# Sixteen early landing places, one modulation path moved between engines, and a feed-forward finish by quarters in a one-core decoder layer

## The chip, the core and the metric

The kernel runs on one core of a Trainium2 chip. TensorE multiplies matrices, VectorE (DVE) and ScalarE (ACT) work elementwise, GpSimd (POOL) here only fills memory with zeros, and SyncE (SP) issues the transfers from main memory. The metric is device time in microseconds (us) of one execution.

## The reference

One layer of a decoder trunk, batch 1, 256 tokens, width 2048, all in float32:

```
mod = silu(c) @ w_ada + b_ada                 # 2048 -> 12288: sh1, sc1, g1, sh2, sc2, g2
h   = rms_norm(x, norm1_g) * (1 + sc1) + sh1
q, k, v, u = split(h @ w_in)                  # 2048 -> 4096
attn = dilated_attention(rms(q), rms(k), v)   # 8 heads of 128, three dilations
y    = gelu(s5(u))                            # 64 groups, 64 complex states, a scan
ssm  = y * sigmoid(y @ w_glu + b_glu)
x    = x + g1 * (concat(rms(attn), rms(ssm)) @ w_out)
h2   = rms_norm(x, norm2_g) * (1 + sc2) + sh2
out  = x + g2 * (relu(h2 @ w_ff1)**2 @ w_ff2) # 2048 -> 8192 -> 2048
```

## The kernel before

**Weights.** All weights stream through once, some 300 MB. A weight tile of 512 KB lands in one of five buffers called raw; ScalarE copies it to wh (a rounded high part), VectorE writes raw - wh to wl, and TensorE computes high x high, high x low and low x high (the split, lines 161 and 136; lines 193 to 195 in the input projection). wh and wl have three buffers each. A part is 1 MB of w_in (two raw tiles, 24 matmuls of 512 columns) or 512 KB of w_out, w_ff1 or w_ff2. A part of the latter is 24 matmuls of 256 columns in `pair_bank` (lines 869 to 872, both outputs in one PSUM bank) or 8 of 512 and 8 of 256 in `pair_part` (lines 860 and 862).

**Modulation.** w_ada, 100 MB, is cut into 24 blocks of four 1 MB pieces; a block gives four columns of 128 of `mod`. `ADA_ORDER` is the order of the blocks. A block in `PE_BLOCKS` goes to TensorE: per piece four matmuls of 32 output columns (line 254), at the end a copy, four transposing matmuls (line 265) and an add into `mod`. Any other block goes to VectorE: each piece is multiplied by silu(c) and summed (line 158); silu(c), copied to all partitions, is the tile cbc, which is loaded and computed near the start. `pump(n)` issues the next n pieces; `pump_at(i)` issues `PUMPS[i]` of them on average at each part of stage i. The first eight pieces land in tiles that are not used yet (Q, K, U, V, and two halves each of TO and CA), later ones in the tags of the current ring (`RINGS`), or in raw in two halves.

**The order of the work.** The text of the program: eight pieces of modulation, small S5 terms, h(0), the input projection in blocks of 512 columns n and groups of 512 rows kg (h(kg) is made by `make_h`), and between its blocks the tables of the S5 branch: `b_step` and `ca_step` on VectorE, `pad_write` copies on ScalarE into the zeroed tiles padB (PD) and padCs (WB0, WB1), `toep_half` (TensorE line 526), `wb_block`. When u is complete, `state_in` and `scan` (VectorE, tiles XT and T0) run beside the rest of the input projection; then `y_block` (lines 697 and 701), attention and w_glu, the output projection from both branches, the second norm (n, line 828 broadcasts it), h2, and the feed-forward. There `ff1_half(0)` and `ff1_half(8)` run the first two groups of rows for 16 column pairs and store the partial sums in part; ff1(0) to ff1(7) finish eight of them pair by pair, then ff1 and ff2 alternate in four groups G.

The compiler orders the instructions of each engine by its own simulation, with the text as priority; every engine then works its queue in that order. `tc.issue_after(x)` keeps instructions behind x.

In the listing, acc and tr are PSUM tiles (four banks each).

Of the kernel before, what the change touches and what calls it, by code (L numbers as in the profile page):

```python
# [9 lines left out]
F32 = mybir.dt.float32  # L10
# [6 lines left out]
P = 128  # L17
# [9 lines left out]
RAW = 5  # L27
RINGS = (('Q', 'K'), ('raw',), ('T0', 'PD', 'raw', 'raw'), ('T0', 'raw', 'raw'), ('raw',), ('HA', 'U', 'WB0'), ('HA', 'PD'))
PUMPS = (2.0, 2.0, 1.0, 1.0, 1.0, 1.0, 1.0, 0.5, 0.5, 2.5, 1.0, 2.0, 1.0, 0.5)

# [10 lines left out]
SUB = [0, 2, 1, 3]  # L41
PE_BLOCKS = (0, 1, 4, 5, 10, 11, 12, 16)
ADA_ORDER = (4, 0, 5, 1, 6, 2, 7, 3, 8, 9, 10, 11, 12, 16, 13, 17, 14, 18, 15, 19, 20, 21, 22, 23)

# [153 lines left out]
def _body(nc, tc, I, out, sb, ps):  # L198
# [14 lines left out]
    c0 = t("T0", [P, 2, 32, 16])  # L213
    cbc = t("cbc", [P, DM])
    ones = t("ones", [P, 1])
# [8 lines left out]
    mod = t("mod", [P, 96])  # L224
    first = [t(tag, [P, 4, NB]) for tag in ("Q", "K", "U", "V")]
    for tag in ("TO", "CA"):
        w = t(tag, [P, 8, NB])
        first += [w[:, 0:4], w[:, 4:8]]

    ring = {"tags": ("raw",), "i": 0, "first": 0}  # L230

    def ada_raw(src):
        if ring["first"] < 8:
            raw = first[ring["first"]]
            ring["first"] += 1
            nc.sync.dma_start(raw, src.rearrange("p (a n) -> p a n", a=4))
            return [raw]
        ring["i"] += 1
        tag = ring["tags"][ring["i"] % len(ring["tags"])]
        if tag not in ("raw", "T0"):  # L240
            raw = t(tag, [P, 4, NB])
            nc.sync.dma_start(raw, src.rearrange("p (a n) -> p a n", a=4))
            return [raw]
        return [k.raw(src[:, 2 * NB * i : 2 * NB * i + 2 * NB].rearrange("p (a n) -> p a n", a=2), tag) for i in range(2)]

    def ada_pieces(b):
# [20 lines left out]
        else:  # L267
            part = t("adap", [P, 2, 4], bufs=2)
            for j in range(4):
                o = 0  # L270
                for i, raw in enumerate(ada_raw(I["w_ada"][b, j])):
                    n = raw.shape[1] * NB
                    rf = raw.rearrange("p a n -> p (a n)")
                    stt(rf, rf, 1.0, cbc[:, o : o + n], ALU.mult, ALU.mult, accum=part[:, i, j : j + 1])
# [42 lines left out]
    def make_h(kg):  # L317
# [3 lines left out]
        for kc in range(4 * kg, 4 * kg + 4):  # L321
            v = xTf[:, kc]
            mul(v, v, rbc)
            nc.scalar.activation(v, v, AF.Identity, bias=mod[:, kc : kc + 1], scale=g1c[:, kc : kc + 1])
            end = k.split(hs[kg][:, 0, kc % 4], hs[kg][:, 1, kc % 4], v)
        return end.ins
# [150 lines left out]

    padB = t("PD", [P, 32, 2, 2, 16])
    padCs = [t(f"WB{i}", [P, 8, 2, 2, 4, 16]) for i in range(2)]
    for w in (padB, *padCs):  # L480
        nc.gpsimd.memset(w, 0.0)
    by_r = lambda v: v.rearrange("p i r j -> p r i j")
# [128 lines left out]
    for i in range(4):  # L611
        sl = slice(NB * i, NB * i + NB)
        sg = t("rows", [P, NB], bufs=2)
        with tc.issue_after(h_act):
            nc.scalar.activation(sg, cbc[:, sl], AF.Sigmoid)
        with tc.issue_after(h_end):
            mul(cbc[:, sl], cbc[:, sl], sg)
    with tc.issue_after(h_act):
# [10 lines left out]
    make_h(1)  # L629
    ring["tags"] = RINGS[1]  # L630
    cw = t("T0", [P, 2, 2, 16, 16])
# [9 lines left out]
    s5_powers()  # L641
    ring["tags"] = RINGS[2]
    run(w_in_pair(4, [0, 1]), 3)
# [4 lines left out]
    make_h(3)  # L648
    ring["tags"] = RINGS[3]
    for n in (0, 1):  # L650
        run(w_in_block(n, [3]), 6)
    ring["tags"] = RINGS[4]
    u2 = t("PD", [P, 2, 32, 32])
# [145 lines left out]
    for n in range(2):  # L799
# [20 lines left out]
        if n == 0:  # L820
            ring["tags"] = RINGS[6]
            att = t("U", [P, NH, SEQ])
# [119 lines left out]
    def ff1_half(base):  # L942
# [7 lines left out]
        for i in range(8):  # L950
            copy(part[base + i], banks[i])

    def ff1(np_):
        pp = [k.acc(), k.acc()]
# [3 lines left out]
        for kg in kgs:  # L958
            pair_part(pp, I["w_ff1"][np_, kg], h2[4 * kg : 4 * kg + 4], kg == kgs[0], kg == 3)
        aa = ff1_slot(np_)  # L960
        v = t("rows", [P, 2, SEQ], bufs=2)
        for e in range(2):
# [70 lines left out]
```

## Time and profile before

| | |
|---|---|
| median of 3 runs | 1297.09 us (1292.63 to 1297.53) |
| the profiled execution | 1291.11 us, span 1289.3 us |
| TensorE (PE) busy | 1193.7 us, 93% of the span |
| weight loads (PEld) | 1012.5 us, 79% |
| VectorE busy | 910.5 us, 71% |
| ScalarE busy | 579.0 us, 45% |
| moved by transfers | 299.64 MB, mean 232 GB/s |
| mean granted TensorE clock | 0.948 of full |

[...] The profile's other views give the same by stretches of time, by line, or as a list in order of time.

### The profile page before, as it was taken

The numbers are of one execution on the slowest core, as the hardware profiler recorded it, in microseconds if no ns is written. First come the engines' busy times: TensorE is split into PE (matmuls) and PEld (weight loads), VectorE is DVE, ScalarE is ACT, GpSimd is POOL, SyncE is SP. The second block draws the span as 40 slices with busy tenths as digits, with TensorE's granted clock in tenths as the row PEclk, the third lists the DMA queues.
The fourth block names the chain that finished last, engine by engine and source line by source line (L and its number), as shares of the span: only waits on it lengthen the run. The fifth ranks groups of instructions, "written<-read, shape, count | busy, mean of one in ns | idle before, by whom it ended". The sixth has DMA issues, their size and how long they took to land.

```text
span 1289.3 us, 18892 instructions
## 1 busy us (share of the span) xinstructions
PE 1193.7 (93%) x7330; PEld 1012.5 (79%) x7330; DVE 910.5 (71%) x1499; ACT 579.0 (45%) x792; POOL 13.0 (1%) x12
## 2 busy tenths in 40 slices
PE   4688899998998799789989999999999999999998
PEld 1456677863777699789978888888888888888887
DVE  5977697899534985668799655975576666667564
ACT  3588644332145544334354444453344443344432
POOL 1100000000000000000000000000000000000000
PEclk9798999997679899989999999999999999999999
DMA  9785898779155665658997666766677666767663
GB/s 371 286 317 186 280 333 287 274 267 385 36 179 180 239 193 175 210 182 297 327 326 252 203 191 216 262 212 182 195 236 240 225 187 190 219 222 227 202 212 95
DMA packets 77705, 299.64 MB, mean 232 GB/s; under 512 B 8624, under 2 KB 10928, under 8 KB 71856
## 3 DMA queue, kind: packets, MB, share of 16 engines
q1 hardware_dynamic: 77616, 298.45, 69.1%
q8 instruction: 57, 0.93, 0.3%
q14 instruction: 32, 0.26, 0.0%
HBM read 296.31 MB, written 2.10 MB: 231 GB/s over the span
## 4 chain that ended last, share of the span: by engine, by line
PE 60%; DMA 15%; DVE 15%; ACT 5%; issue 4%; SPq 0%; ACTq 0%; DVEq 0%
PE acc L860 31%; PE acc L862 15%; DMA raw<-w_ada 10%; DVE wl L136 4%; DVE raw L158 3%; DVE T L136 2%; PE acc L872 2%; PE acc L870 2%; PE acc L869 2%; PE acc L701 1%; DMA raw<-w_ff 1%; ACT wh L161 1%; PE acc L697 1%; DVE XT L136 1%; ACT TO L161 1%
## 5 line engine op out<-in xcount | busy, mean ns | idle before, releaser
L161 ACT ACTIVATE wh<-raw 128x1024 fp32r<-128x1024 f32 x360 | 381.3, 1060 | 502.1 <-PE acc L860 290.8
L136 DVE TENSOR_TENSOR wl<-raw,wh 128x1024 fp32r<-128x1024 f32 x360 | 439.7, 1223 | 219.0 <-ACT wh L161 217.2
L158 DVE SCALAR_TENSOR_TENSOR raw<-raw,cbc 128x1024 f32<-128x1024 f32 x98 | 119.6, 1225 | 49.3 <-DMA raw<-w_ada 49.0
L860 PE MATMUL acc<-CA,wh 128*128 128x512 f32 x512 | 139.7, 398 | 6.4 <-DVE rows L136 3.4
L860 PEld LDWEIGHTS acc<-CA,wh 128*128 128x128 f32 x512 | 88.4, 190 | 19.2 <-ACT wh L161 4.5
L862 PEld LDWEIGHTS acc<-CA,wl 128*128 128x128 f32 x512 | 76.7, 189 | 10.7
L862 PE MATMUL acc<-CA,wl 128*128 128x256 f32 x512 | 78.2, 278 | 0.0
L860 PE MATMUL acc<-WB,wh 128*128 128x512 f32 x256 | 70.2, 396 | 0.0
L860 PE MATMUL acc<-TO,wh 128*128 128x512 f32 x256 | 70.0, 394 | 0.0
L193 PE MATMUL acc<-wh,HA 128*128 128x512 f32 x128 | 49.8, 417 | 13.2 <-ACT HA L161 9.2
L194 PE MATMUL acc<-wl,HB 128*128 128x512 f32 x128 | 52.6, 411 | 7.1 <-DVE wl L136 7.0
L194 PE MATMUL acc<-wl,HA 128*128 128x512 f32 x128 | 53.2, 416 | 0.9 <-DVE wl L136 0.9
L195 PE MATMUL acc<-wh,HB 128*128 128x512 f32 x128 | 50.6, 400 | 0.0
L195 PE MATMUL acc<-wh,HA 128*128 128x512 f32 x128 | 50.5, 406 | 0.0
L193 PE MATMUL acc<-wh,HB 128*128 128x512 f32 x128 | 47.5, 403 | 1.7 <-ACT wh L161 1.7
L860 PEld LDWEIGHTS acc<-WB,wh 128*128 128x128 f32 x256 | 43.5, 188 | 5.6
L860 PEld LDWEIGHTS acc<-TO,wh 128*128 128x128 f32 x256 | 43.4, 188 | 5.5
L862 PEld LDWEIGHTS acc<-WB,wl 128*128 128x128 f32 x256 | 39.1, 188 | 5.9
L862 PEld LDWEIGHTS acc<-TO,wl 128*128 128x128 f32 x256 | 38.9, 188 | 5.8
L193 PEld LDWEIGHTS acc<-wh,HA 128*128 128x128 f32 x128 | 25.1, 198 | 22.4 <-ACT HA L161 9.3
L862 PE MATMUL acc<-WB,wl 128*128 128x256 f32 x256 | 40.8, 281 | 0.0
L862 PE MATMUL acc<-TO,wl 128*128 128x256 f32 x256 | 39.8, 277 | 0.0
(322 smaller groups left out, 2352.0 us busy)
## 6 DMA issues: line engine op xcount, KB each, us to landing
raw<-w_ff SPq DMA_DIRECT2D x256, 512.0 KB, 4.3
raw<-w_ada SPq DMA_DIRECT2D x98, 512.0 KB, 5.2
raw<-w_in SPq DMA_DIRECT2D x64, 512.0 KB, 6.0
raw<-w_out SPq DMA_DIRECT2D x32, 512.0 KB, 3.8
HA<-w_ada SPq DMA_DIRECT2D x11, 1024.0 KB, 7.3
PD<-w_ada SPq DMA_DIRECT2D x9, 1024.0 KB, 4.9
Q<-w_ada SPq DMA_DIRECT2D x5, 1024.0 KB, 10.3
K<-w_ada SPq DMA_DIRECT2D x5, 1024.0 KB, 8.7
```

What stands on the lines that cost most here:

```text
L136: return (eng or self.nc.vector).tensor_tensor(out, a, b, op=op)
L158: self.nc.vector.scalar_tensor_tensor(out, a, s, b, op0=op0, op1=op1, accum_out=accum)
L161: self.last_act = self.nc.scalar.activation(out, a, AF.Copy, scale=scale).ins
L193: mm(ps, xh, wh, start=start, stop=False)
L194: mm(ps, xh, wl, start=False, stop=False)
L195: mm(ps, xl, wh, start=False, stop=stop)
L697: mm(pv[:, r - r8], toep[:, r].rearrange("p g s j -> p (g s j)"), u2[:, :, r, :], start=True, stop=False)
L860: mm(pp[e], hi[:, e, kk], xs[kk].rearrange("p s n -> p (s n)"), start=first and kk == 0, stop=False)
L862: mm(pp[e][:, 0:SEQ], lo[:, e, kk], xs[kk][:, 0], start=False, stop=last and kk == 3)
L869: mm(o, hi[:, e, kk], xs[kk][:, 0], start=first and e + kk == 0, stop=False)
L870: mm(o, hi[:, e, kk], xs[kk][:, 1], start=False, stop=False)
L872: mm(o, lo[:, e, kk], xs[kk][:, 0], start=False, stop=last and e + kk == 4)
```

## The change

1. `FIRST` names sixteen landing places in place of eight (WB0, WB1, PD, and Q, K, TO and CA a second time). The pumps of the first two w_in parts are 4 instead of 2, so pieces 9 to 16 follow there. The zeroing of padB and padCs comes after them.
2. Blocks 2, 3, 6 and 7 join `PE_BLOCKS`: all of norm1's modulation (blocks 0 to 7) is on TensorE. Blocks 10, 11, 12 and 16 move ahead of 8 and 9.
3. cbc is only needed from block 8 on: it is loaded, and its sigmoid and product computed, after the last w_in part; until then the tag cbc is a landing place.
4. `make_h` multiplies by scale and norm in one VectorE operation, ScalarE adds the shift and rounds to the high part, VectorE gives the low part: three operations per chunk in place of four.
5. The S5 tables' loads and steps stand after two w_in parts instead of one.
6. `ff1_rest` finishes the first eight column pairs group by group: the third group of rows of all eight, then the fourth, in eight PSUM banks. The pump of the feed-forward's first half is 0.4 instead of 0.5, and ff1's own pump no longer runs for these eight.

```diff
+FIRST = ("Q", "K", "U", "V", "TO", "TO", "CA", "CA", "WB0", "WB1", "PD", "Q", "K", "TO", "TO", "CA")
-RINGS = (('Q', 'K'), ('raw',), ('T0', 'PD', 'raw', 'raw'), ('T0', 'raw', 'raw'), ('raw',), ('HA', 'U', 'WB0'), ('HA', 'PD'))
-PUMPS = (2.0, 2.0, 1.0, 1.0, 1.0, 1.0, 1.0, 0.5, 0.5, 2.5, 1.0, 2.0, 1.0, 0.5)
+RINGS = (("cbc", "K"), ("cbc", "PD", "raw", "raw"), ("cbc", "raw", "raw"), ("HA", "U", "WB0"), ("HA", "PD"))
+PUMPS = (4.0, 2.0, 1.0, 1.0, 0.75, 0.5, 1.0, 0.5, 0.5, 2.5, 1.0, 2.0, 1.0, 0.4)
-PE_BLOCKS = (0, 1, 4, 5, 10, 11, 12, 16)
-ADA_ORDER = (4, 0, 5, 1, 6, 2, 7, 3, 8, 9, 10, 11, 12, 16, 13, 17, 14, 18, 15, 19, 20, 21, 22, 23)
+PE_BLOCKS = (0, 1, 2, 3, 4, 5, 6, 7, 10, 11, 12, 16)
+ADA_ORDER = (4, 0, 5, 1, 6, 2, 7, 3, 10, 11, 12, 16, 8, 9, 13, 17, 14, 18, 15, 19, 20, 21, 22, 23)
...
             v = xTf[:, kc]
-            mul(v, v, rbc)
-            nc.scalar.activation(v, v, AF.Identity, bias=mod[:, kc : kc + 1], scale=g1c[:, kc : kc + 1])
-            end = k.split(hs[kg][:, 0, kc % 4], hs[kg][:, 1, kc % 4], v)
+            sh = mod[:, kc : kc + 1]
+            stt(v, v, g1c[:, kc : kc + 1], rbc, ALU.mult, ALU.mult)
+            hi = hs[kg][:, 0, kc % 4]
+            k.last_act = nc.scalar.activation(hi, v, AF.Identity, bias=sh).ins
+            end = nc.vector.scalar_tensor_tensor(
+                hs[kg][:, 1, kc % 4], v, sh, hi.bitcast(F32), op0=ALU.add, op1=ALU.subtract
+            )
...
-padB = t("PD", [P, 32, 2, 2, 16])
+    run(w_in_block(0, [0]), 0)
+    run(w_in_block(1, [0]), 0)
     ring["tags"] = RINGS[0]
-    run(w_in_block(0, [0]), 0)
+    padB = t("PD", [P, 32, 2, 2, 16])
+    padCs = [t(f"WB{i}", [P, 8, 2, 2, 4, 16]) for i in range(2)]
+    for w in (padB, *padCs):
+        nc.gpsimd.memset(w, 0.0)
     for w in range(2):
         nc.sync.dma_start(bpow[w][:, 3], I["bb"][:, w])
     nc.sync.dma_start(c0, I["cc"])
...
-    run(w_in_block(1, [0]), 0)
     nc.sync.dma_start(idents, I["consts"][:, 0 : P + 32])
-    nc.sync.dma_start(cbc, I["cbc"])
...
-    ring["tags"] = RINGS[5]
+    ring["tags"] = RINGS[3]
+    cbc = t("cbc", [P, DM])
+    nc.sync.dma_start(cbc, I["cbc"])
+    for i in range(4):
+        sl = slice(NB * i, NB * i + NB)
+        sg = t("rows", [P, NB], bufs=2)
+        nc.scalar.activation(sg, cbc[:, sl], AF.Sigmoid)
+        mul(cbc[:, sl], cbc[:, sl], sg)
+    vec["c"] = cbc
...
+    def ff1_rest(base):
+        banks = [tr() for _ in range(4)] + [k.acc() for _ in range(4)]
+        for kg in range(2, 4):
+            make_h2(kg)
+            for i in range(8):
+                pair_bank(banks[i], I["w_ff1"][base + i, kg], h2[4 * kg : 4 * kg + 4], kg == 2, kg == 3)
+                pump_at(13, 80)
+        for i in range(8):
+            v = t("rows", [P, 2, SEQ], bufs=2)
+            add(v.rearrange("p e n -> p (e n)"), banks[i], part[base + i])
+            ff1_square(v, base + i)
...
     ff1_half(8)
-    make_h2(2)
-    make_h2(3)
-    for np_ in range(8):
-        ff1(np_)
+    ff1_rest(0)
```

## Rows read from the trace of the kernel before

**Rows 1.** Stages: us; PE, PEld, DVE, ACT, POOL busy (instructions); PE clock, DMA share, GB/s.
```profile
46.40:140.00 93.60, 82.83 (x494) 61.26 (x495) 70.82 (x118) 77.23 (x142) 1.81 (x1) 0.90 0.69 244
140.00:227.50 87.50, 80.36 (x338) 62.86 (x336) 71.05 (x104) 39.99 (x54) 0.22 (x1) 0.96 0.85 302
227.50:329.20 101.70, 91.50 (x470) 62.87 (x471) 96.77 (x157) 34.87 (x42) 0.00 (x0) 0.90 0.81 298
329.20:427.40 98.20, 88.99 (x673) 73.63 (x673) 41.10 (x97) 41.76 (x84) 0.00 (x0) 0.72 0.38 134
427.40:538.50 111.10, 106.66 (x880) 104.79 (x880) 81.68 (x137) 51.18 (x74) 0.00 (x0) 0.98 0.63 204
538.50:552.40 13.90, 2.33 (x13) 1.93 (x12) 9.39 (x24) 2.11 (x5) 0.00 (x0) 0.69 0.67 220
552.40:656.00 103.60, 95.13 (x768) 93.04 (x768) 79.40 (x130) 44.18 (x58) 0.00 (x0) 0.96 0.81 278
656.00:715.70 59.70, 57.39 (x319) 49.76 (x320) 58.74 (x102) 28.99 (x35) 0.00 (x0) 0.97 0.83 274
715.70:1289.30 573.60, 568.67 (x3267) 495.86 (x3265) 371.52 (x496) 242.63 (x273) 0.00 (x0) 1.00 0.66 206
```

**Rows 2.** One stretch for line 195's instructions alone; columns PE and PEld as above.
```profile
46.40:227.50 181.10, 72.73 (x184) 35.97 (x184) 0.93 0.77 272
```

**Rows 3.** Timeline: start us, duration, engine, line, operation, output and inputs, [idle before, releaser].
```profile
36.10 1.05 PE L265 MATMUL tr<-ones,rows 128*128 128x1 f32 x8 [0.72 <-ACT rows L161]
...
37.27 4.44 DVE L136 TENSOR_TENSOR XT<-XT,rbc 128x256 f32<-128x256 f32 x13
...
43.77 0.15 DVE L136 TENSOR_TENSOR mod<-tr,small 128x4 f32<-128x4 f32 x1
...
45.94 1.32 ACT L161 ACTIVATE HA<-XT 128x256 fp32r<-128x256 f32 x4
...
46.40 0.80 PE L193 MATMUL acc<-wh,HA 128*128 128x512 f32 x1 [9.24 <-ACT HA L161]
```

**Rows 4.** Timeline of TensorE around 80 us.
```profile
78.00 0.39 PE L193 MATMUL acc<-wh,HA 128*128 128x512 f32 x1
78.23 0.39 PE L194 MATMUL acc<-wl,HA 128*128 128x512 f32 x1
...
79.57 1.96 PE L526 MATMUL tr<-WB,PD 128*32 128x128 f32 x64
...
85.55 1.04 PE L254 MATMUL tr<-K,cpad 128*32 128x512 f32 x8
86.40 1.04 PE L254 MATMUL tr<-Q,cpad 128*32 128x512 f32 x8
```

**Rows 5.** Stretches for line 158's instructions alone: us, DVE busy (instructions), clock, DMA.
```profile
46.40:227.50 181.10, 44.60 (x68) 0.93 0.77 272
227.50:329.20 101.70, 13.58 (x20) 0.90 0.81 298
```

**Rows 6.** Timeline of TensorE at the first output matmul of the state-space branch.
```profile
329.22 0.45 PE L701 MATMUL acc<-XT,CA 64*64 64x64 f32 x8 [1.47 <-DVE XT L136]
```

**Rows 7.** Groups by line and shape, VectorE: busy us, mean ns, idle before.
```profile
L136 DVE TENSOR_TENSOR cbc<-cbc,rows 128x512 f32<-128x512 f32 x4 | 2.7, 686 | 5.6 <-ACT rows L615 5.6
```

**Rows 8.** Timeline at the start: GpSimd and VectorE.
```profile
2.47 3.55 POOL L481 MEMSET WB<- 128x2048 f32 x2
...
3.02 3.03 DVE L152 TENSOR_SCALAR HA<-small 128x32 f32<-128x32 f32 x1 [1.42 <-DMA small<-small]
```

**Rows 9.** Timeline of VectorE in the attention stage.
```profile
419.90 2.29 DVE L158 SCALAR_TENSOR_TENSOR PD<-PD,cbc 128x2048 f32<-128x2048 f32 x1 [2.95 <-DMA PD<-w_ada]
```

**Rows 10.** Timeline of VectorE and TensorE before the second sub-layer.
```profile
546.57 1.23 DVE L158 SCALAR_TENSOR_TENSOR raw<-raw,cbc 128x1024 f32<-128x1024 f32 x1 [2.04 <-DMA raw<-w_ada]
...
549.64 1.20 PE L828 MATMUL tr<-ident,n 128*128 128x128 f32 x4 [5.74 <-DVE n L136]
```

**Rows 11.** Ten microseconds of the output projection, columns as in rows 1.
```profile
500.00:510.00 10.00, 10.00 (x88) 10.00 (x87) 5.20 (x7) 4.45 (x5) 0.00 (x0) 1.00 0.50 145
```

More of the change, by code (lines that the diff above doesn't have):

```diff
@@ L213, in _body @@
     c0 = t("T0", [P, 2, 32, 16])
-    cbc = t("cbc", [P, DM])
     ones = t("ones", [P, 1])
@@ L224, in _body @@
     mod = t("mod", [P, 96])
[L225 to L228, printed above, removed]
+    halves = {}
+    vec = {}
     ring = {"tags": ("raw",), "i": 0, "first": 0}
     def ada_raw(src):
-        if ring["first"] < 8:
-            raw = first[ring["first"]]
+        if ring["first"] < len(FIRST):
+            tag = FIRST[ring["first"]]
+            if tag in ("TO", "CA"):
+                if tag in halves:
+                    raw = halves.pop(tag)[:, 4:8]
+                else:
+                    halves[tag] = t(tag, [P, 8, NB])
+                    raw = halves[tag][:, 0:4]
+            else:
+                raw = t(tag, [P, 4, NB])
             ring["first"] += 1
@@ L273, in ada_pieces @@
                     rf = raw.rearrange("p a n -> p (a n)")
-                    stt(rf, rf, 1.0, cbc[:, o : o + n], ALU.mult, ALU.mult, accum=part[:, i, j : j + 1])
+                    stt(rf, rf, 1.0, vec["c"][:, o : o + n], ALU.mult, ALU.mult, accum=part[:, i, j : j + 1])
                     o += n
@@ L475, in pad_write @@
             copy(dst(gp)[pr], src[pr])
-    padB = t("PD", [P, 32, 2, 2, 16])
-    padCs = [t(f"WB{i}", [P, 8, 2, 2, 4, 16]) for i in range(2)]
-    for w in (padB, *padCs):
-        nc.gpsimd.memset(w, 0.0)
     by_r = lambda v: v.rearrange("p i r j -> p r i j")
@@ L607, in _body @@
             ca_step(d, cw[:, 0], cw[:, 1])
-    run(w_in_block(1, [0]), 0)
     nc.sync.dma_start(idents, I["consts"][:, 0 : P + 32])
-    nc.sync.dma_start(cbc, I["cbc"])
[L611 to L617, printed above, removed]
     with tc.issue_after(h_act):
@@ L629, in _body @@
     make_h(1)
-    ring["tags"] = RINGS[1]
     cw = t("T0", [P, 2, 2, 16, 16])
@@ L641, in _body @@
     s5_powers()
-    ring["tags"] = RINGS[2]
+    ring["tags"] = RINGS[1]
     run(w_in_pair(4, [0, 1]), 3)
@@ L648, in _body @@
     make_h(3)
-    ring["tags"] = RINGS[3]
     for n in (0, 1):
         run(w_in_block(n, [3]), 6)
-    ring["tags"] = RINGS[4]
+    ring["tags"] = RINGS[2]
     u2 = t("PD", [P, 2, 32, 32])
@@ L820, in _body @@
         if n == 0:
-            ring["tags"] = RINGS[6]
+            ring["tags"] = RINGS[4]
             att = t("U", [P, NH, SEQ])
@@ L951, in ff1_half, with ff1_square @@
             copy(part[base + i], banks[i])
+    def ff1_rest(base):
[9 more added lines that the diff above has]
+            ff1_square(v, base + i)
+    def ff1_square(v, np_):
+        aa = ff1_slot(np_)
+        stt(v, v, 0.0, v, ALU.max, ALU.mult)
+        copy(aa[:, :, 0], v)
+        sub(aa[:, :, 1], v, aa[:, :, 0].bitcast(F32))
     def ff1(np_):
@@ L959, in ff1 @@
             pair_part(pp, I["w_ff1"][np_, kg], h2[4 * kg : 4 * kg + 4], kg == kgs[0], kg == 3)
-        aa = ff1_slot(np_)
         v = t("rows", [P, 2, SEQ], bufs=2)
@@ L967, in ff1 @@
             add(v[:, e], pp[e][:, 0:SEQ], v[:, e])
-        stt(v, v, 0.0, v, ALU.max, ALU.mult)
-        copy(aa[:, :, 0], v)
-        sub(aa[:, :, 1], v, aa[:, :, 0].bitcast(F32))
+        ff1_square(v, np_)
     def ff2(G, np_):
```

## The prediction

> **What bounds the kernel now.** I first read the stage windows [rows 1]. They split the 1289.3 us span into two halves of a different kind. From 715.7 us on TensorE is busy 568.7 of 573.6 us at full clock: nothing in this change takes matmuls out of there, so a gain must come from the 715 us ahead of it. There no engine is full throughout. Up to 140 us ScalarE leads (77.2 of 93.6 us, the state-space tables), from 140 to 227.5 us nobody (TensorE 80.4, VectorE 71.1 of 87.5, transfers at 0.85), and from 227.5 to 329.2 us VectorE is full: 96.8 of 101.7 us.
>
> Then the windows restricted to one line. Line 195 runs eight times per part (512 rows by 512 columns) of the input projection; its 184 instructions up to 227.5 us are 23 of the 32 parts [rows 2], and two dense matmuls start 0.23 us apart, so a part costs 24 x 0.23 = 5.5 us [rows 4]. 23 parts are 127 of 181.1 us; the rest is table work, modulation and waiting. Line 158, VectorE's modulation reduction, takes 44.6 us of VectorE in that stretch and 13.6 us in the next [rows 5]. The timeline then says what ends the next stretch: the first output matmul of the state-space branch waits until 329.22 us for VectorE's last XT operation, the scan [rows 6].
>
> **The change part by part.** Its own base is the profiled execution, 1291.1 us for a span of 1289.3, so 1.8 us lie around the span. The timed runs are 1292.6 to 1297.5, median 1297.1: the profile is 6 us under the median, and I add 2 us to the sum for that.
>
> *Start and h.* The last modulation column needed by the first h is in PSUM at 36.10 + 1.05 = 37.15 us, but the VectorE add that stores it starts at 43.77, 6.6 us later, behind sixteen XT products (thirteen in the row, three more) and two weight splits [rows 3]. After, a product needs the scale of its own group, so only the first four can stand there: four at 4.44/13 = 0.34 us are 1.4 us. The splits may stay (128x1024 like the 1.23 us reduction of rows 10). The matmul at 46.40 also loses one of three ScalarE/VectorE passes behind that add, 1.32 us for four copies [rows 3]. Bounds 0 and -8; I take **-6**, nearest to the queue's length. The same copies saved for the other twelve chunks (4 us of ScalarE) lie beside weight splits; I count nothing.
>
> *Sixteen landing places, modulation on TensorE, up to the complete u.* Pieces 16 to 31 (blocks 6, 2, 7, 3) go from VectorE to TensorE, and blocks 10 and 11 move ahead of 8 and 9. TensorE had 8 pieces in 46.4 to 227.5 us; by the pump counts it gets 27 (35 less the first 8). Two neighbouring pieces start 0.85 us apart [rows 4]: 19 x 0.85 = +16 us. VectorE loses all 44.6 us of line 158, and the 1 MB pieces no longer wait in its queue. Lower bound of the stretch: 127 us of parts, 27 x 0.85 = 23, tables two times 2 x 1.96 us [rows 4], say 158 against 181, -23; upper bound +16, if the idle time stays. The first half is ScalarE's, which loses only sigmoids and copies; the second has 7 us of idle TensorE and 16 us of idle VectorE. So TensorE's addition about eats the relief: **-2**.
>
> *From u to the scan's end.* VectorE's 96.8 us lose 13.6 us of line 158 [rows 1, 5]. They gain four sigmoid products, 2.7 us [rows 7], since cbc is now loaded here; 96.8 - 13.6 + 2.7 = 86 us. TensorE needs 9 parts x 5.5 = 50 us, about 13 pieces (11 us) and the state matmuls, so it stays below. Of the 15.8 us difference I take **-14**; bounds 0 (transfers of the pieces decide) and -16.
>
> *Moves on queues.* On SP, the tables bb and cc go behind eight 1 MB pieces and a second w_in part. On GpSimd three memsets leave the start and wait for pieces 8 to 10; behind them stand the toep memsets. What waits for both is the table work, whose cover is the matmuls of further parts. Cost 0 while those are ahead in TensorE's queue; if not, see the last rival. The memset itself: at the start a VectorE operation on 32 columns took 3.03 us and ended at 6.05, with the GpSimd memsets' end at 2.47 + 3.55 = 6.02 us [rows 8]. After, the same memsets run in the middle of VectorE's work: 0 to 5.4 us (three at 1.78); I take 0, since nearly all of VectorE's work there is products of two tensors.
> [...]
>
> *Attention and output projection (329.2 to 538.5 us).* Blocks 8 and 9 are now reduced on VectorE here, eight pieces at 2.29 us [rows 9] = 18 us more, and TensorE loses eight. VectorE is busy 41.1 of 98.2 us up to 427.4 [rows 1], so there is room; the hazard is that a reduction holds up what stands behind it, as at 419.90, after 2.95 us of waiting for its transfer [rows 9]. Bounds -8 (the TensorE pieces were in the way as well) and +24; I take **0**.
>
> *Before the second sub-layer.* TensorE idles 13.9 us, and 5.74 us of it is the wait for n, which stands behind a reduction that itself waits 2.04 us for its transfer at 546.57 [rows 1, 10]. Before, piece 64 is pumped at the sixth of eight output pairs, after at the fourth, about 11 us earlier (four parts of 24 matmuls at 88 in 10 us, 2.73 us each [rows 11]). **-5**; bounds 0 and -7.
>
> *First half of the feed-forward.* 32 parts x 2.73 = 87.3 us took 103.6 us [rows 1, 11], 16.3 us too long, at 278 GB/s. The pump of 0.4 instead of 0.5 fetches 12.8 pieces instead of 16: 3.4 MB less, 12 us at that rate. Bounds 0 and -16; **-10**.
>
> *Finish by quarters.* h2's last group is needed eight parts later than its third. 656 to 715.7 us holds 319 matmuls, 20 parts of 16, 54.6 us at 2.73; 5.1 us are lost [rows 1]. The bank form has 24 matmuls of 256 columns instead of 8 of 512 and 8 of 256, the same columns. **-3**; bounds +2 and -5. VectorE's one wide add for four narrow ones is off the path.
>
> *What is left over.* Four pieces fewer are pumped between the feed-forward pairs, so block 23's four come at once ahead of the last 32 parts: eight reductions of 1.23 us [rows 10] and 4.2 MB through the five raw buffers, against eight parts (22 us) ahead in buffers. **+2**; bounds 0 and +6.
>
> Sum: -6 -2 -14 +0 -5 -10 -3 +2 = -38. 1291.1 - 38 + 2 = **1255 us**.
>
> **The rivals.**
> *TensorE takes over the front.* The 16 us of pieces come on top: the first stretch is +10 instead of -2, and the scan's end gains 8 instead of 14, since TensorE is not done. For it: TensorE is busy 91.5 of 101.7 us up to 329.2 [rows 1]; against: part of that busy time is pieces filling a wait. Sum -20: **1273 us**.
> *The front runs free.* With VectorE's reductions gone the waits behind them go too: -15 for -2, the feed-forward's 15 for 10, and 6 in the attention. -62: **1231 us**. Against it stands ScalarE up to 140 us.
> *Reductions clog the attention.* All eight on the path, and two waits as in rows 9: 18.4 + 5.9 = +24, sum -14: **1279 us**; with a wait for each, 42 us, no gain at all.
> [...]
> *Tables too late (slower).* bb and cc come 9.4 MB later on SP, 31 us at 302 GB/s [rows 1]. If the toeplitz matmuls, at 79.57 us now [rows 4], go to 110 us and stand in TensorE's queue ahead of the next w_in part, TensorE idles from the end of two parts and eight pieces (40.4 + 11 + 7 = 58 us): 52 us, sum +14: **1307 us**. It decides from 38 us of idle on. Against it: before, they also stand later than the text puts them, for 33 us from 46.4 to 79.57 hold more than five parts, and only two precede them in the text.
>
> **How the numbers follow.** The forecast 0.46 (its own range 1240 to 1272), TensorE 0.20, free front 0.13, clogged attention 0.11, late tables 0.10. This kernel's runs tell 0.5% (6.5 us) from no change. Faster: 0.46 + 0.20 + 0.13 + 0.07 of the clogged attention = 0.86; same: 0.04 of it and 0.03 of the late tables = 0.07; slower 0.07. The range 1228 to 1290 holds the forecast, TensorE, most of the clogged attention and half of the free front, 0.81.
>
> **What would show it.** The first w_in matmul at 40 to 41 us; no line 158 before the last w_in part; u complete near 219 us with 27 pieces between; the first matmul of line 701 near 307 us, still behind VectorE's XT; the gap before the second sub-layer near 9 us; the feed-forward's first 32 parts in 93 us; a last stretch as long as now. I am wrong if TensorE idles over 10 us ahead of line 526 (tables), if line 701 waits for TensorE's own queue (front), or if line 158's waits between 329 and 430 us sum to over 10 us.

## The result: slower, and the profile after

The change made the kernel slower, by 1.5%: median 1315.28 us (1312.4 to 1319.53, 4 runs) against 1297.31 us, ratio 1.0148 with a 95% interval of 1.011 to 1.0186. The forecast was 1255. Ratios here and below leave disturbed runs out, so one can differ from that of the plain medians. The profiled execution took 1312.4 us, its span 1310.6. Its stage windows, cut at the events of [rows 1] (columns as there; here the first matmul of the input projection is at 39.6, u is complete at 242.6, the state-space output begins at 327.6, the output projection at 439.9, the feed-forward at 556.1, the ninth column pair at 715.7; in [rows 1] the last cut lies four parts behind the start of the ninth pair, which is at 704.6):

```profile
39.60:120.00 80.40, 60.85 (x393) 39.55 (x394) 52.01 (x82) 52.37 (x93) 12.58 (x7) 0.90 0.67 260
120.00:242.60 122.60, 119.10 (x589) 82.21 (x587) 52.19 (x66) 59.79 (x89) 0.22 (x1) 1.00 0.70 251
242.60:327.60 85.00, 85.00 (x458) 63.22 (x456) 75.12 (x112) 29.56 (x35) 0.00 (x0) 1.00 0.68 232
327.60:439.90 112.30, 85.97 (x700) 71.89 (x699) 87.08 (x157) 56.45 (x101) 0.00 (x0) 0.79 0.70 264
439.90:556.10 116.20, 108.08 (x884) 106.29 (x884) 74.08 (x136) 53.30 (x78) 0.00 (x0) 0.96 0.51 163
556.10:663.00 106.90, 97.14 (x767) 94.99 (x768) 70.70 (x110) 44.41 (x57) 0.00 (x0) 0.96 0.74 242
663.00:715.70 52.70, 47.23 (x387) 46.00 (x386) 40.97 (x62) 22.43 (x27) 0.00 (x0) 1.00 0.81 269
715.70:1306.60 590.90, 584.54 (x3326) 509.43 (x3327) 393.38 (x535) 248.37 (x281) 0.00 (x0) 1.00 0.65 210
```

From 120 us to the complete u TensorE is now full (119.1 of 122.6 us) and VectorE not even half (52.2): the front changed its bound. The stretch from the first matmul to u is 203.0 us, before 227.5 - 46.4 = 181.1. It holds 22 parts of w_in where it held 23 [rows 2] (176 matmuls of line 196 against 184 of line 195), so one part went to the next stretch. The modulation pieces on TensorE in it, eight matmul records each, before (line 254) and after (line 260), columns PE and PEld:

```profile
46.40:227.50 181.10, 8.95 (x64) 1.59 (x64) 0.93 0.77 272
39.60:242.60 203.00, 29.97 (x208) 5.61 (x208) 0.96 0.69 255
```

These are 8 pieces before and 26 after. The scan stretch fell from 101.7 to 85.0. In the attention VectorE went from 41.1 to 87.1 us, and the stage from 98.2 to 112.3.

Why the front has a hole besides, the timelines of TensorE and VectorE show around 70 us:

```profile
52.86 2.36 DVE L137 TENSOR_TENSOR V<-T,sm 128x1024 f32<-128x1024 f32 x2
...
67.59 1.06 PE L260 MATMUL tr<-CA,cpad 128*32 128x512 f32 x8
...
68.73 1.29 DVE L137 TENSOR_TENSOR CA<-V 128x512 f32<-128x512 f32 x2 [1.33 <-PE tr L260]
...
82.37 1.29 DVE L137 TENSOR_TENSOR CA<-V 128x512 f32<-128x512 f32 x2
...
83.70 3.44 ACT L162 ACTIVATE WB<-CA 64x768 f32<-64x768 f32 x4 [6.91 <-DVE CA L137]
...
85.50 3.64 PE L532 MATMUL tr<-WB,PD 128*32 128x128 f32 x64 [9.86 <-issue]
```

CA is landing place 16. The table ca shares its memory: the products that it is made from (V) are done at 55.2 us, and its first write comes at 68.73, when TensorE has read that piece. The last table product ends near 83.7 us, and only then does ScalarE copy CA into WB, which the toeplitz matmuls read. TensorE stands idle for 9.86 us ahead of them, a wait for which the profile names no releaser; they then take 3.64 us for the work that took 1.96 in [rows 4]. They start 45.9 us after the first matmul, before 33.2.

In the attention, the same windows for line 159's instructions alone (VectorE's modulation reduction; columns us, busy, clock, DMA):

```profile
327.60:378.20 50.60, 9.20 (x8) 0.78 0.77 302
378.20:439.90 61.70, 27.46 (x24) 0.80 0.65 232
```

Each reduction gives two records, so these are 16 reductions, 36.7 us; before there was one, 2.3 us. The timeline of VectorE ahead of the output projection:

```profile
422.62 2.29 DVE L159 SCALAR_TENSOR_TENSOR PD<-PD,cbc 128x2048 f32<-128x2048 f32 x1 [1.90 <-DMA PD<-w_ada]
...
430.98 2.29 DVE L159 SCALAR_TENSOR_TENSOR PD<-PD,cbc 128x2048 f32<-128x2048 f32 x1 [3.51 <-DMA PD<-w_ada]
433.19 0.08 DVE L159 DVE_READ_ACCUMULATOR PD<-PD,cbc 128x1 f32 x1
433.19 0.15 DVE L153 TENSOR_SCALAR rs<-tr 128x2 f32<-128x2 f32 x1
...
433.70 2.29 DVE L159 SCALAR_TENSOR_TENSOR HA<-HA,cbc 128x2048 f32<-128x2048 f32 x1
```

The 0.15 us step rs, from which the branch's norm and with it the output projection follow, stands behind a reduction that waits 3.51 us for its transfer; a second reduction comes in the middle of the norm. The list of waits gives TensorE's line 836, the broadcast of that norm, 7.0 us of waiting for rs.

In the feed-forward's first half the waits are (us in total, times, longest; the first line is that of the kernel before, 552.4 to 656 us, where the reduction is line 158):

```profile
DVE raw L158 <- DMA raw<-w_ada: 11.7, 11, 3.0
DVE raw L159 <- DMA raw<-w_ada: 32.0, 13, 4.1
ACT wh L162 <- DMA raw<-w_ff: 24.1, 9, 5.0
```

And near the end, the burst that is left over (SP's transfers, then TensorE):

```profile
1193.63 14.20 SPq L179 DMA_DIRECT2D raw<-w_ada  x8
1208.65 6.18 SPq L179 DMA_DIRECT2D raw<-w_ff  x5
1215.77 2.86 PE L868 MATMUL acc<-V,wh 128*128 128x512 f32 x6 [4.39 <-ACT wh L162]
```

### The profile page after: what moved, and what is told of

It is laid out like the page before. It is cut to its first block, busy times and chain, and to the rows that moved or that the text cites. A ratio compares the mean times of both kernels' runs of the same rounds, so it can differ in the third digit from the quotient of the medians.

```text
span 1310.6 us, 19312 instructions
## 1 busy us (share of the span) xinstructions
PE 1210.9 (92%) x7618; PEld 1020.9 (78%) x7618; DVE 867.9 (66%) x1383; ACT 579.7 (44%) x783; POOL 13.1 (1%) x12
## 4 chain that ended last, share of the span: by engine, by line
PE 69%; DMA 11%; DVE 6%; ACT 5%; issue 4%; DVEq 0%; ACTq 0%; SPq 0%
PE acc L868 27%; PE acc L870 14%; DMA raw<-w_ada 8%; PE acc L195 4%; PE acc L194 4%; PE acc L196 3%; PE tr L260 3%; PE acc L878 2%; PE acc L877 2%; PE acc L880 2%; DVE wl L137 2%; DMA PD<-w_ada 2%; DVE raw L159 1%; ACT wh L162 1%; PE tr L556 1%
## 5 line engine op out<-in xcount | busy, mean ns | idle before, releaser
L159 DVE SCALAR_TENSOR_TENSOR raw<-raw,cbc 128x1024 f32<-128x1024 f32 x64 | 78.2, 1224 | 63.2 <-DMA raw<-w_ada 62.7
L868 PE MATMUL acc<-CA,wh 128*128 128x512 f32 x384 | 104.6, 396 | 1.7 <-DVE rows L137 0.9
L868 PEld LDWEIGHTS acc<-CA,wh 128*128 128x128 f32 x384 | 65.9, 188 | 11.0 <-issue 1.1
L870 PEld LDWEIGHTS acc<-CA,wl 128*128 128x128 f32 x384 | 58.2, 188 | 8.3
L870 PE MATMUL acc<-CA,wl 128*128 128x256 f32 x384 | 60.4, 281 | 0.0
L877 PE MATMUL acc<-CA,wh 128*128 128x256 f32 x192 | 48.3, 284 | 0.2 <-ACT CA L162 0.2
L878 PE MATMUL acc<-CA,wh 128*128 128x256 f32 x192 | 47.8, 282 | 0.0
```

Source lines behind the costliest of these rows:

```text
L159: self.nc.vector.scalar_tensor_tensor(out, a, s, b, op0=op0, op1=op1, accum_out=accum)
L868: mm(pp[e], hi[:, e, kk], xs[kk].rearrange("p s n -> p (s n)"), start=first and kk == 0, stop=False)
L870: mm(pp[e][:, 0:SEQ], lo[:, e, kk], xs[kk][:, 0], start=False, stop=last and kk == 3)
L877: mm(o, hi[:, e, kk], xs[kk][:, 0], start=first and e + kk == 0, stop=False)
L878: mm(o, hi[:, e, kk], xs[kk][:, 1], start=False, stop=False)
```

## The experiments

Fifteen kernels ran, in five jobs, each beside runs of the kernel before on the same chip: medians of 1296.3, 1294.8, 1294.5, 1295.8 and 1297.0 us. Single runs of it spread from 1276.7 to 1303.0, so a total under 1% off says little by itself; where a cause rests on a stretch, the profile is given.

**Four parts undone one at a time, from the changed kernel.**

Four blocks back on VectorE, sixteen places kept:
```
-PE_BLOCKS = (0, 1, 2, 3, 4, 5, 6, 7, 10, 11, 12, 16)
+PE_BLOCKS = (0, 1, 4, 5, 10, 11, 12, 16)       # cbc made early, rings without cbc
```


> The changed kernel, with blocks 6, 2, 7 and 3 (pieces 16 to 31) reduced on VectorE again and the sigmoid product of c made early again; the sixteen landing places, h in three steps and the finish by quarters stay. Theory 'TensorE has taken over the front': the front loses 16 pieces of 0.85 to 1.0 us on TensorE, first w_in matmul to complete u (203 us) shrinks by 14 to 20, the scan stretch (85) grows by about 14 as it did before; the total comes out at 1305 to 1315. Theory 'tables too late': the toeplitz matmuls still start near 85 us, the front stays at 200 us or more, and with the scan stretch back at 100 the total is 1325 or more.


1294.14 us, ratio 0.9997 (0.9963 to 1.0031). The front took 191.0 us and the scan stretch 87.6, although the toeplitz matmuls came still later (96.16 us, TensorE idle for 16.88). Neither theory came out: the front lost 12.0 us where 14 to 20 or none were expected, and the total is lower than both. Another 9.2 us of the gain lie in the attention (103.1 us), where neither had put any. The scan stretch did not need the four blocks on TensorE, which neither theory said either.

Tables early, twelve places:
```
-FIRST = (..., "PD", "Q", "K", "TO", "TO", "CA")
+FIRST = (..., "PD", "Q")
     run(w_in_block(0, [0]), 0)
-    run(w_in_block(1, [0]), 0)     # moved behind the toeplitz tables' loads and steps
```


> The changed kernel with twelve landing places instead of sixteen and the tables' loads, memsets and steps put between the first and the second w_in part, as before the change; TensorE still does all of blocks 0 to 7. Theory 'tables too late': the toeplitz matmuls start near 75 us instead of 85.5, TensorE's idle stretch of 10 us ahead of them goes, u is complete 8 to 12 us earlier, total near 1305. Theory 'TensorE has taken over the front': TensorE has the same work to do, u comes at most 4 us earlier, total 1311 to 1316.


1296.24 us, ratio 1.0017 (0.9997 to 1.0037), 19 us off. Its windows from the first matmul to u, to the state-space output, to the output projection:

```profile
40.70:235.80 195.10, 178.32 (x980) 121.38 (x980) 104.41 (x147) 112.11 (x182) 6.13 (x5) 0.97 0.72 263
235.80:321.50 85.70, 85.70 (x456) 63.31 (x454) 75.22 (x112) 29.75 (x35) 0.00 (x0) 1.00 0.68 235
321.50:423.20 101.70, 85.54 (x715) 73.23 (x713) 86.42 (x158) 61.24 (x110) 0.00 (x0) 0.84 0.76 287
```

The front lost 7.9 us, TensorE's idle stretch ahead of the tables is gone. (Against the 12.0 us of the first run this is near what one profile can tell, so the two do not rank TensorE's load and the late tables.) But 10.6 us of the gain lie in the attention, where neither theory had put any: with twelve places instead of sixteen, the ring of landing tags starts there at another of its three tags.

Blocks 8 and 9 on TensorE:
```
-PE_BLOCKS = (0, ..., 7, 10, 11, 12, 16)
+PE_BLOCKS = (0, ..., 7, 8, 9, 10, 11, 12, 16)
```


> The changed kernel with blocks 8 and 9 on TensorE too, so that VectorE has no reduction between the complete u and the output projection. Theory 'reductions clog the attention': the wait of the w_out rstd behind the PD reductions (TensorE idle from 424 to 436.7) goes, the first w_out part starts 8 to 12 us earlier (428 to 432 instead of 439.9), total 1303 to 1307. Rival 'the transfers are what is late': TensorE now waits for the same 1 MB pieces itself, the first w_out part stays within 3 us of 439.9, total 1312 or more.


1313.53 us, ratio 1.0142 (1.0123 to 1.0161): against the changed kernel's 1315.28 nothing, and the attention took 108.8 us for 112.3, with 3 reductions in it instead of 16. "Reductions clog the attention" does not explain the loss by itself; the wait on rs is still 4.4 us.

The burst spread by doubled pumps:
```
-            pump(1)
+            pump(2 if np_ % 6 == 2 else 1)     # in ff1
```


> The changed kernel with four pieces more pumped between the feed-forward pairs (every third call pumps two), so that none is left for a burst ahead of the last 32 parts. Theory 'the burst costs': the last 208 parts take 582 to 584 us instead of 591, the total is 7 to 9 us shorter, 1306 to 1308. Rival 'the burst is hidden, the last stretch is longer for another reason': the stretch stays at 588 or more, total 1312 or more.


1318.94 us, ratio 1.0177 (1.0162 to 1.0192). The burst's place was mended: the 64 matmuls from the 568th to the 504th from the end took 11.2 us instead of 17.9 (before 11.1). But the doubled pumps cost the same elsewhere: 820 to 920 us had TensorE busy 94.6 of 100, where the changed kernel had 99.1 from 811 to 911. Nothing won, for a reason that the expectation did not hold.

**The attention ring alone, and the pace.**
```
-RINGS = (..., ("HA", "U", "WB0"), ("HA", "PD"))
+RINGS = (..., ("U", "WB0", "HA"), ("HA", "PD"))
```


> The changed kernel with one line changed: the attention ring is turned by one place, ('U', 'WB0', 'HA') for ('HA', 'U', 'WB0'), so that its pieces land in the order WB0, HA, U again, as before the change and as with twelve landing places; sixteen landing places had shifted its start. Theory 'the eleventh piece lands in WB0, which the branch needs for its own squares': from the first state-space output matmul to the first w_out part 98 to 103 us instead of 112, total 1300 to 1307. Rival 'the shift is harmless, the attention of the run with early tables was shorter because its transfers ran earlier': the stretch stays at 109 or more, total 1311 or more.


1307.32 us, ratio 1.0104 (1.0043 to 1.0165): 8 us off by a turned tuple, in medians of different jobs whose intervals overlap; in the profiles the attention took 105.5 us, 6.8 less. It is not the wait that the expectation named: in the changed kernel the piece in WB0 is reduced by 392.33 us, and the branch's first square, which shares that memory, starts only at 400.60, after a wait for VectorE. Most of the difference lies ahead of w_glu. That stretch took 50.6 us and now takes 45.2:

```profile
326.70:371.90 45.20, 40.18 (x407) 29.02 (x406) 36.29 (x62) 18.82 (x30) 0.00 (x0) 0.85 0.79 307
```

In the changed kernel ScalarE goes back and forth between the exponentials of the attention (line 741) and the gelu of the state-space output (line 799) there, and loads a function table each time, four times from 365.63 to 375.47 us. The last:

```profile
375.47 1.28 ACT L799 ACT_TABLE_LOAD   x1
```

With the turn three of the four gelu operations follow the first two loads, and the other two loads come between the third and the last. Why the turn changes that order is not shown.

```
-PUMPS = (..., 0.4)
+PUMPS = (..., 0.5)
```


> The changed kernel with a pace of 0.5 instead of 0.4 pieces per part in the feed-forward's first half: four pieces more in its 32 parts, none in the quarters. If fewer pieces save transfer time there, as predicted (0.75 us per part and 0.1 piece): the first half grows by 10, the quarters lose what they save, total 1313 to 1320. If the pace of 0.4 itself makes VectorE's reductions wait ahead of the weights (40 us of waits in 16 reductions after, 12.7 us in 13 before): start of the second sub-layer to the ninth pair 152 to 155 instead of 159.6, total 1307 to 1311.


1310.69 us, ratio 1.0123 (1.0049 to 1.0197). Windows of the first half and the quarters, and the waits in the first:

```profile
564.20:669.20 105.00, 98.72 (x769) 96.43 (x769) 76.96 (x124) 43.69 (x57) 0.00 (x0) 0.95 0.77 266
669.20:715.40 46.20, 45.94 (x385) 45.74 (x386) 34.62 (x44) 22.30 (x27) 0.00 (x0) 1.00 0.72 241
```
```profile
ACT wh L162 <- DMA raw<-w_ff: 27.9, 14, 5.5
DVE raw L159 <- DMA raw<-w_ada: 16.8, 11, 3.5
```

With more pieces VectorE waits 16.8 us at the head of its queue instead of 32.0, but the first half is only 2 us shorter (105.0 against 106.9). The larger part is in the quarters, 46.2 us against 52.7: at 0.5 all sixteen pieces are fetched in the first half, and none is left for the quarters. The total by itself is not clear of the changed kernel's. All seven profiles with the pace 0.4 need 159 to 162 us from the start of the feed-forward to the ninth pair; the eight with 0.5 and the quarters need 145 to 154.

**Parts of the change alone, on the kernel before.** The finish by quarters:
```
-    make_h2(2); make_h2(3)
-    for np_ in range(8):
-        ff1(np_)
+    ff1_rest(0)
```


> The kernel before with the finish by quarters alone (ff1_rest in place of the eight pairs; pumps as before, so that no piece is fetched in it and four are left for a burst ahead of the last 32 parts). If the quarters themselves are slower than the pairs (the bank form's 24 matmuls of 256 columns, narrow results late): start of the second sub-layer to the ninth pair 156 or more instead of 152 us, and with the burst's 6 us the total is 1306 or more. If the form costs nothing and the pieces paced at 0.4 were what stretched it: 146 to 150 us, the burst gives 6 back, total 1295 to 1301.


1290.59 us, ratio 1.0038 (0.998 to 1.0096), no difference that can be told. The windows of its first half and its quarters:

```profile
556.00:657.40 101.40, 95.61 (x769) 93.71 (x769) 77.00 (x124) 43.59 (x57) 0.00 (x0) 0.96 0.79 275
657.40:701.50 44.10, 43.86 (x384) 43.67 (x385) 34.33 (x44) 22.22 (x27) 0.00 (x0) 1.00 0.72 248
```

145.5 us in all, before 152.2 (552.4 to the ninth pair at 704.6). In its own stretch, 44.1 us for 48.6, the form gains 4.5 us without pieces in it, and the burst (17.9 us for the 64 matmuls) takes it back.

h in three steps alone, `make_h` as in the change:
```
-            mul(v, v, rbc)
-            nc.scalar.activation(v, v, AF.Identity, bias=..., scale=...)
-            end = k.split(hi, lo, v)
+            stt(v, v, g1c[:, kc : kc + 1], rbc, ALU.mult, ALU.mult)
+            nc.scalar.activation(hi, v, AF.Identity, bias=sh)
+            end = nc.vector.scalar_tensor_tensor(lo, v, sh, hi, ...)
```


> The kernel before with h in three steps alone. If the three ScalarE/VectorE passes are what holds the first input-projection matmul at 46.4 us: it starts at 40 to 42 us, and the total is 4 to 6 us shorter (1289 to 1292 against about 1295). If the start is held by the queue of products ahead (the four-step form is not it), or the front gives the gain back behind the tables: first matmul earlier but complete u still at 226 to 228 us, total within 2 us of before.


1280.81 us, ratio 0.9891 (0.984 to 0.9941). The first matmul at 39.36 us, u 178.7 us after it. More than expected in the totals; in the profiled spans it is 4.5 us.

Both of these, and the burst's pieces spread otherwise:
```
     def ff2(G, np_):
+        if G < 2 and np_ in (2, 5):
+            pump(1)
```


> The kernel before with three parts of the change that are off the front's modulation: h in three steps, the finish by quarters, and the four pieces left over fetched one by one during the first two G rounds' output pairs instead of in a burst. If the gains stand side by side: finish by quarters 1290.6, less 4 to 6 for the start, less 6 for the burst, 1277 to 1282. If the start's gain is given back behind the tables or the spread pieces cost as much where they are now: 1286 or more.


1275.87 us, ratio 0.984 (0.9785 to 0.9896). The 64 matmuls take 11.1 us again. Placed in `ff2`, the four pieces cost little: the last stretch, from the ninth pair on, is 586.7 us, before 584.7.

**What cost time, undone together, from the changed kernel.** The edits of the first two runs:
```
 # PE_BLOCKS as in the first run; FIRST and the tables as in the second
```


> The two edits that each took about 20 us off, together: blocks 6, 2, 7, 3 reduced on VectorE and the tables between the first and the second w_in part with twelve landing places (which also turns the attention ring back). If TensorE's modulation load and the late tables are two separate losses in the front: first w_in matmul to complete u 181 to 186 us (191 and 195 with one edit each), total 1272 to 1282. If both edits remove the same wait (TensorE's idle stretch ahead of the toeplitz matmuls): the front stays at 190 or more, and only the ring's part comes on top, total 1283 to 1290.


1293.56 us, ratio 1.0001 (0.997 to 1.0033): no gain over either edit. Together they do not add up, and the front still took 189.2 us (in a profile that fell on the slowest of its executions, 1302.3 us).

The four blocks on VectorE, ring, pace and spread pieces:
```
 # PE_BLOCKS as in the first run; RINGS turned; PUMPS ending in 0.5; pump(1) in ff2
```


> The changed kernel with the four things that the runs so far say cost time undone: blocks 6, 2, 7, 3 on VectorE, the attention ring turned back, the pace 0.5, and the four pieces of the burst fetched one by one in the first two G rounds. If they add up: 1294 less 5 to 8 (ring), less 4 (pace), less 6 (burst), 1275 to 1280. If VectorE's reductions and the ring remove the same wait: 1284 to 1288.


1277.01 us, ratio 0.9874 (0.9848 to 0.99), as the sum said. Its attention, for line 159's instructions alone (columns us, busy, clock, DMA, GB/s), and the wait for rs in it:

```profile
317.10:415.40 98.30, 36.70 (x32) 0.87 0.78 295
```
```profile
412.27 1.22 PE L838 MATMUL tr<-ident,rs 128*128 128x128 f32 x4 [8.10 <-DVE rs L137]
```

That is the same 36.7 us of reductions as in the changed kernel and as long a wait for rs, in a stage of 98.3 us, as long as before. So neither the sixteen reductions nor that wait makes the stage long by itself.

The tables early, pace and spread pieces:
```
 # FIRST and the tables as in the second run; PUMPS ending in 0.5; pump(1) in ff2
```


> The changed kernel with modulation of the first sub-layer still all on TensorE, twelve landing places and the tables early, the pace 0.5 and the four pieces of the burst fetched one by one. If pace and burst add to the tables' gain: 1296 less 4.6 less 6, 1284 to 1288. If it stays at 1292 or more, the pace's gain was TensorE idle time that late pieces fill anyway.


1278.72 us, ratio 0.9899 (0.9864 to 0.9934): with all of the first modulation on TensorE. Pace and burst together gave 17.5 us over the run with early tables, more than the 10.6 expected.

**Order, engine and place, one at a time.** On the 1276 us kernel: first `ADA_ORDER` of the change alone (with one piece more pumped ahead of the attention and the attention ring turned, so that pieces land there as before), then also its `PE_BLOCKS`; last, the old order with blocks 8 and 9 on TensorE.
```
-ADA_ORDER = (4, 0, 5, 1, 6, 2, 7, 3, 8, 9, 10, 11, 12, 16, ...)
+ADA_ORDER = (4, 0, 5, 1, 6, 2, 7, 3, 10, 11, 12, 16, 8, 9, ...)   # both
 # both too: RINGS' ("HA", "U", "WB0") to ("WB0", "HA", "U"); the ninth of PUMPS 0.5 to 1.0
-PE_BLOCKS = (0, 1, 4, 5, 10, 11, 12, 16)
+PE_BLOCKS = (0, 1, 2, 3, 4, 5, 6, 7, 10, 11, 12, 16)             # the second only
```


> The 1276 us version (before with h in three steps, quarters, spread pieces) with the order of the change alone: blocks 10, 11, 12, 16 ahead of 8 and 9, engines as before (one piece more ahead of attention, its ring turned so that pieces land as before). If the scan stretch got shorter after the change because blocks 8 and 9 left VectorE there: complete u to first state-space output matmul 85 to 90 us instead of 102, complete u near 178 to 182 us after the first input-projection matmul, total 1258 to 1268. If it got shorter because TensorE took blocks 6, 2, 7, 3: stretch 98 or more, total 1274 or more.

> The same, with blocks 6, 2, 7 and 3 on TensorE as well, so that all of the first sub-layer's modulation is TensorE's, but with eight landing places and the tables where they were before. If TensorE's pieces simply add (16 of about 1 us): first input-projection matmul to complete u 192 to 198 us, total 12 to 18 over the run with the order alone. If the relief of VectorE was hidden by the late tables, as the prediction would have it: 178 to 184 us, total at most 3 over it.


1266.55 us, ratio 0.9773 (0.9717 to 0.9829), and 1295.63 us, ratio 1.0006 (0.9984 to 1.0028). First matmul to complete u, without and with the four blocks on TensorE; and for each, line 254 (a modulation piece on TensorE; columns PE and PEld) alone. The order alone:

```profile
39.70:215.00 175.30, 157.38 (x820) 117.60 (x820) 141.89 (x222) 111.40 (x182) 2.90 (x3) 0.95 0.79 288
39.70:215.00 175.30, 12.56 (x80) 2.27 (x80) 0.95 0.79 288
```

With the engine moved too:

```profile
40.40:250.00 209.60, 185.96 (x984) 126.84 (x986) 106.09 (x151) 114.64 (x186) 2.03 (x2) 0.92 0.69 244
40.40:250.00 209.60, 34.24 (x210) 6.06 (x212) 0.92 0.69 244
```

VectorE is relieved of 35.8 us and TensorE gets 21.7 us of pieces (16, so 1.35 us each), and the stretch grows by 34.3: TensorE's busy time by 28.6, its idle time by 5.7. With more landing places the same move costs less. With sixteen places it is 12.0 us (191.0 to 203.0), with twelve and early tables 5.9 (189.2 to 195.1), for 17 us more of pieces in each, so there the relief gave back some 5 and 11 us. The order's scan stretch is 84.5 us with the four blocks on VectorE. But it is given back: the attention of the order alone, state-space output to w_glu and on to the output projection, took 55.9 and 68.9 us:

```profile
299.50:355.40 55.90, 9.15 (x8) 0.69 0.73 268
355.40:424.30 68.90, 27.52 (x24) 0.78 0.63 223
```

Line 158's 16 reductions are there again, but only four of them in the first of the two stretches, and TensorE is not waiting in it:

```profile
299.50:355.40 55.90, 53.53 (x442) 36.88 (x441) 32.30 (x55) 14.46 (x24) 0.00 (x0) 0.69 0.73 268
```

TensorE is busy 53.53 of 55.90 us at a granted clock of 0.69. Why this attention is 124.8 us long stays open; its profile is that of the slowest of the run's executions (1274.0 us).

```
-PE_BLOCKS = (0, 1, 4, 5, 10, 11, 12, 16)
+PE_BLOCKS = (0, 1, 4, 5, 8, 9, 10, 11, 12, 16)
```


> The 1276 us version with blocks 8 and 9 on TensorE where they stand (before u is complete and in the scan stretch), order, places and everything else as there. If VectorE's 13.6 us of reductions are what the scan stretch can lose, and the attention's 16 reductions are what the order cost again: the stretch from complete u to the first state-space output matmul takes 86 to 92 us instead of 101.7, the attention stays at 97 to 99, total 1262 to 1267. If TensorE's 8 us of pieces eat it: stretch 98 or more, total 1273 to 1277.


1265.07 us (1263.48 to 1269.19), ratio 0.9779 (0.9695 to 0.9862), the lowest median, 50 us under the changed kernel; from the run with the order alone (1266.55 us) it cannot be told. Its windows to u, to the state-space output, to the output projection:

```profile
41.00:214.40 173.40, 155.72 (x820) 116.50 (x820) 141.53 (x223) 111.50 (x182) 2.95 (x3) 0.96 0.80 288
214.40:306.80 92.40, 90.42 (x465) 65.24 (x464) 81.94 (x126) 33.93 (x41) 0.00 (x0) 0.96 0.68 244
306.80:405.40 98.60, 87.68 (x770) 67.49 (x769) 45.01 (x104) 48.37 (x91) 0.00 (x0) 0.89 0.61 227
```

The scan stretch is 9.3 us shorter than with blocks 8 and 9 on VectorE (101.7), and nothing is given back in the attention, 98.6 us (before 98.2). The gain of 10.8 us in the medians is not clear of the noise by itself; the stretch shows it.

## Why the prediction was wrong, by its own steps

| step | said | profile | verdict |
|---|---|---|---|
| start and h | -6 | -6.8 | right |
| up to the complete u | -2 | +21.9 | failed |
| u to the scan's end | -14 | -16.7 | right |
| attention, output projection | 0 | +14.1 and -4.6 | failed |
| before the second sub-layer | -5 | -4.2 | right in size, by another wait |
| first half of the feed-forward | -10 | +3.3 | failed in sign |
| finish by quarters (to the ninth pair) | -3 | +4.1 | form right, pieces in it not counted |
| left over (from the ninth pair) | +2 | +10.2 | mis-sized |

**Up to the complete u.** The step that failed is "So TensorE's addition about eats the relief: -2". The stretch grew by 21.9 us, past the step's upper bound of +16 for a front whose idle time stays. The 18 pieces more took 21.0 us of TensorE (29.97 - 8.95), 1.17 us each, where 0.85 was put. TensorE's idle time, which the relief of VectorE was to shrink, rose instead: from 17.9 us (181.1 less 163.2 busy) to 23.1. One part fewer takes 5.5 us off; the remaining 1.3 us are spread over the other work. So the relief came out at nothing here, though not in every pair of kernels: the same move cost 34.3 us with eight landing places, 12.0 with sixteen and 5.9 with twelve and early tables. The prediction read [rows 1] as a front in which no engine is full, and concluded that VectorE's 44.6 us were half of what held it; but TensorE was busy 163.2 of 181.1 us before. The rival "TensorE takes over the front" (+10) came nearest and was priced too low. The rise in idle time is that of the tables: 9.86 us of idle TensorE ahead of them, gone in the run with early tables, whose front is 7.9 us shorter (its total is 11 us under that of the run with the ring alone, whose attention pieces land alike). That rival was set to decide from 38 us of idle on; it acted from the first, and through CA, landing place 16, which the prediction never followed to its next owner. Late tables do not always hurt: with the four blocks on VectorE, sixteen places and late tables gave 1277.0 us. What the number of places does by itself is not separated, since these kernels differ in rings, pumps and the tables' place too.

**u to the scan's end.** Right in size, and for the reason given: line 158's reductions there, blocks 8 and 9, are gone. Two kernels show that their leaving is enough (84.5 us with the order alone, 92.4 with 8 and 9 on TensorE). Two parts of the step's reasoning did not hold: VectorE is busy 75.1 us there and not 86, and TensorE, which was to stay below, is busy 85.0 of 85.0 us, with ten parts instead of nine.

**Attention.** The step was 0, because VectorE had room by its busy time; it measured +14.1. It added eight reductions, and sixteen came: with 8 and 9 later, eight pieces of the blocks behind them were reduced ahead of the output projection's start too, that were reduced behind it before (there the reductions fall from 23.4 to 4.9 us). Its own sign, over 10 us of waits of the reduction, was met: 11.4 us in the stage. But the sixteen reductions by themselves do not make the loss: with three of them the stage took 108.8 us, and another kernel has all sixteen and the same wait for rs in 98.3. What is shown is the tag in which the attention's pieces land, decided by how many pieces had landed earlier: the turned ring takes 6.8 of the 14.1 us off. The ledger has no term for it. The rest stays open. What the rival feared, a step held up by the reduction ahead of it, is there in the row at 430.98: line 774's matmuls, which rs reads, end at 429.76, and rs (0.15 us) starts at 433.19, behind a reduction that waited 3.51 us for its transfer.

**Before the second sub-layer.** The gap fell from 13.9 to 9.7 us, near the forecast, but the wait that the step meant to remove stayed: n still stands behind reductions, and TensorE waits 4.22 us for it, before 5.74.

```profile
553.30 1.22 PE L836 MATMUL tr<-ident,n 128*128 128x128 f32 x4 [4.22 <-DVE n L137]
```

Most of the gain is in the wait ahead of it, 1.63 us for 4.26. So the size was in part luck.

**Feed-forward.** "Fewer pieces, less transfer, -10" took the half to be bound by bytes. The half got longer at 242 GB/s, where it had 278 before, so bytes were not the limit. The step that failed is that fewer pieces save their transfer time. What the trace shows in its place is VectorE standing with a reduction at the head of its queue for a piece that had not landed, 32.0 us where it was 11.7; but the pace of 0.5 halves these waits and takes only 2 us off the half, so they are not the whole of it, and what limits the half stays open. The quarters' own form gains 4.5 us without pieces; the pace of 0.4 left pieces over that fell into it, and made it 52.7 us instead of 46.2. Why 0.4 makes the waits longer than 0.5 (the order that the compiler chose, or the raw buffers' turn) was not separated.

**Left over.** 6.8 of the 10.2 us are the burst (17.9 against 11.1 us for 64 matmuls); with its pieces fetched one by one in `ff2` the last stretch is 2 us longer than before. The other 3.4 us were not traced.

**The sum.** Turning the ring back (8), tables early (11), pace and spread pieces (17.5) bring the changed kernel from 1315.3 to 1278.7 us, in steps of medians from different jobs; the intervals of the ring's step and of the pace's alone overlap with the changed kernel's. The wins of the change were h in three steps, the quarters, and moving 8 and 9 out of VectorE's scan stretch; these three, 8 and 9 going to TensorE and the burst's pieces spread over `ff2`, gave 1265.

## What to carry to other kernels

Busy time that is freed counts only on the engine that ends the stretch last; ask first what the receiving engine has left there (17.9 us of 181.1 here, for 21.0 us of pieces). A landing place has a next owner, and a ring that counts pieces moves every later piece when an early one is added: follow both to the tile that they delay. Background pieces that a slower pace leaves over do not vanish: here they landed in the next stretch, where they cost 6 us, and the half that they were to relieve got no shorter. And a long wait next to a long stage is not yet its cause: look for a run that has the wait without the length.

## What the runs showed of the hardware

The time of a modulation piece on TensorE depended on where it stood. One alone takes 1.04 us at a granted clock of 1.00 (85.5 to 87.5 us), and two neighbours start 0.85 us apart [rows 4]; on average a piece took 1.12 us in the front before, 1.15 after, and 1.35 for the sixteen that the move with eight landing places added, where from 80 to 120 us the granted clock was 0.83. In the stretch of the state-space output the granted clock was 0.50 before (333 to 366 us), with TensorE busy 32.9 of 33.0 us in matmuls of 64 columns and one modulation piece near the end. After, with five pieces between them, it was 0.78 (327.6 to 378.2 us), and the eight-matmul groups took 0.62 us each where it was 0.50 (339.3 to 348.5) and 0.38 where it was 1.00 (350 to 362), though the stage did not get shorter. The kernel with the spread pumps has the same order of instructions as the changed kernel up to the feed-forward, and its profile reached u 207.6 us after the first matmul, not 203.0: one profile tells a stretch to some 5 us. The GpSimd fill of TO (5.48 us from 64.62) lay beside VectorE's products of two tensors, which took 1.29 us for two then (68.73) and 1.29 us at 82.37 without it; before, products of XT started 0.34 us apart beside a fill (37.3 to 39.3 us) and 0.34 us apart without it (39.3 to 41.6). No wait shows there, and the 0 us taken for it stood; what made the 3.03 us of [rows 8] is not shown.
